# A decoder layer with an expert lookup on one core: three half sums in their own SBUF tile, and more gate, u and row buffers

## The chip, the core and the metric

The kernel runs on one core of one Trainium2 chip. The core has five engines that each take their own instructions strictly in order and signal each other through semaphores: TensorE (PE in the rows; PEld is its weight load), VectorE (DVE), ScalarE (ACT), GpSimd (POOL) and SyncE (SP, which here only issues DMAs). POOL issues DMAs too, the gathers by row number among them. The metric is device time in microseconds from start to end of one execution, the median of several; lower is better.

## The reference

One transformer layer over 1024 tokens of width 1024: modulated norm, windowed attention with a short convolution beside it, then a lookup of 16,384 experts, and a last norm. The lookup is what the change touches:

```python
def chunk(t):                                         # peer(), cut
    qh = (t @ w_q).reshape(T, 8, 2, 128)
    s = einsum('thpd,hpnd->thpn', qh, sub_keys)       # 2 x 128 scores a head
    s_top, i_top = top_k(s, 16)
    cand = s_top[:, :, 0, :, None] + s_top[:, :, 1, None, :]
    best, pos = top_k(cand, 16)                       # 16 of 256 pairs
    idx = take_along_axis(cand_idx, pos)              # rows of u_tab, v_tab
    g = softmax(best)
    act = gelu(einsum('thkd,td->thk', u_tab[idx], t))
    return einsum('thk,thkd->td', g * act, v_tab[idx])
...
x = x + g2 * peer(h2, ...);  return rmsnorm(x, final_g)
```

Each token takes 8 x 16 = 128 of the 16,384 rows of u_tab and v_tab.

## The kernel before

All matrix products are made in float16 pairs: a float32 operand is split into a high half (ACT, a scaled copy) and a low half (DVE, the rest), and `mm3` makes three matmuls of each product: high by high, high by low, low by high. Names ending in h and l (uh and ul, vh and vl, wdh and wdl) are such halves.

The run has three parts.

**The front** (up to about 1122 us): norms, projections, attention, convolution, mixing, and then, for each half of 512 tokens, the query projection and the top-k of the scores on DVE (`stage2`, `scores`; results in sv and si). While half 1 goes through `stage2`, the gates of half 0 are built beside it (`gates`): `select` finds the 16 pairs of each head, and `build_g` turns them into a dense table of gate values: DVE writes one-hot tiles e1, e2, ah, al of 8 tokens, `expand` multiplies them on PE, four tokens to a PSUM bank, ACT moves each bank into a tile ge (line 994), and each full ge goes to the table gd in DRAM. The weights of this part live in the pool wts, 24 KB per partition: four buffers whl and two w32 (`weight`). Its last user is the u part of chunks 3 to 5, which `run` splits ahead (`u_first`); their matmuls are `ups<-h,whl` in the rows.

**hf0** (about 1122 to 2580 us) takes half 0 densely against all experts, in 128 chunks of 128 experts (`chunk`). A chunk loads u (u32) and v (v32) from DRAM, splits them into uh, ul, vh, vl, multiplies uh and ul with the tokens (24 matmuls into a bank ups), applies the gelu (ACT, gel), multiplies by the gate values (DVE, `gel<-gel,gt`) and splits the product into wdh and wdl. Four chunks make a group; with the four v and w parts of one group `outputs` then makes eight blocks d of 128 output columns, two after each chunk of the next group. Blocks 0 to 4 keep their sums in PSUM for all of hf0; blocks 5 to 7 take a bank vps each time, which DVE adds to acc (`acc<-acc,vps`). Only three PSUM banks, v, serve vps, ups and the fbank of `expand`. The gate values come in as tiles gt, two for each block of 8 chunks (q 0 and 1, one for each half of the token blocks), loaded at the head of `chunk` with three buffers.

Beside hf0, `run_side` weaves in side work, a share after each step. It selects the pairs of the four quarters of half 1, and takes `dots` of each quarter: 128 gathered rows of u (POOL, `row`, four buffers), each multiplied with the token's own row and summed by one DVE instruction (`row<-row,hn`). It builds the gate table of the first three quarters.

**hf1** (about 2580 to 3110 us) takes those three quarters, 384 tokens, against v alone (their gates are already multiplied with the activations), chunk groups from the last to the first; the last quarter is summed from 128 gathered rows of v beside it (`rows_out`, racc). Then come the last norms and the output.

Pools stand on a left and a right stack. On the left, above the constants, the pool acc follows where wts has been, and the pool dense0 (gt, u32 and v32, uh, ul, vh, vl, wdl, gel) follows acc. A framework orders the instructions of each engine, places the tiles and inserts the semaphores: a tile that takes over another's memory waits for the last user of that.

Of the kernel before, what the change touches and what calls it, by code (L numbers as in the profile page):

```python
# [8 lines left out]
F32 = mybir.dt.float32  # L9
F16 = mybir.dt.float16  # L10
# [8 lines left out]
D = 1024  # L19
# [8 lines left out]
TB = 8  # L28
# [7 lines left out]
GR = 8  # L36
DVE_ROWS = ((), tuple(range(8)), (), (1, 2, 3, 4, 5, 7))
# [72 lines left out]
class K:  # L110
    def __init__(self, tc, a):
        self.tc = tc
        self.nc = Core(tc.nc)
        self.a = a
        self.wsplit = {}
        self.sel = {}
        self.ndots = {}
        self.nbank = 8
        self.nrstd = 3
        self.waiting = []  # L120
        self.turned = None
# [64 lines left out]
    def setup(self):  # L186
# [34 lines left out]
        self.sv = [None, pc.tile([128, 4, 2, 8, 16], F32, name="sv1")]  # L221
        self.si = [None, pc.tile([128, 4, 2, 8, 16], U32, name="si1")]
# [85 lines left out]
    def square(self, ps, k, x, p, n, tag="sq"):  # L308

        nc = self.nc  # L310
        sq = p.tile([128, n], F32, name=tag, tag=tag, bufs=self.nsq)
# [589 lines left out]
    def row(self, tab, ci, s):  # L901

        r = self.pg.tile([128, D], F32, name="row", tag="row", bufs=4)
# [48 lines left out]
    def build_g(self, t, hf):  # L952
# [7 lines left out]
        for q in range(128 // 16):  # L960
            ge = p.tile([128, 128, 16], F32, name="ge", tag="ge", bufs=self.ge_bufs)
            for sub in range(16 // TB):
# [3 lines left out]
                def onehot(name, src, idx, op):  # L966
                    x = p.tile([128, TB, 128 // REP, REP], F16, name=name, tag=name, bufs=2)
# [16 lines left out]
    def expand(self, t, hf, q, sub, ge, ah, al, e2):  # L984

        nc = self.nc
        for r in range(0, TB, 4):
# [6 lines left out]
            nc.scalar.activation(ge[:, :, o:o + 4].rearrange("p i t -> p t i"), ps, AF.Copy, scale=2.0 ** -12)  # L994
# [8 lines left out]
    def open_gate(self, name, side, ge_bufs):  # L1003
# [4 lines left out]
        io32 = p.tile([128, 128], F32, name="io32")  # L1008
# [65 lines left out]

    def chunk(self, hf, i1, p, pv):
# [5 lines left out]
        if self.gblock != (hf, i1 // GR):  # L1081
            self.gblock = hf, i1 // GR
            self.gts = []
            for q in range(2):
                gt = p.tile([128, nb, GR, 16], F32, name="gt", tag="gt", bufs=3)
                nc.sync.dma_start(
                    gt.rearrange("p b i t -> p b (i t)"),
                    self.gd[hf][nb * q:nb * q + nb].rearrange("b p i t -> p b (i t)")
                    [:, :, i1 // GR * GR * 16:(i1 // GR + 1) * GR * 16])
                self.gts.append(gt)  # L1090
# [51 lines left out]
    def outputs(self, hf, gi, d, chunks, acc, pv):  # L1142

        nc = self.nc
        nt = (NDENSE, NMIX)[hf]
# [11 lines left out]
        po = po[:, :nt]  # L1157
# [3 lines left out]
        ad = acc[:, d, :nt]  # L1161
        if keep:
            if last:
                nc.scalar.activation(ad, po, AF.Copy)
        elif first:
            nc.vector.tensor_copy(ad, po)
        else:
            nc.vector.tensor_add(ad, ad, po)
# [20 lines left out]
    def dense(self, p, pv, accs):  # L1189

        self.res, self.mix, self.vparts, self.gblock = {}, {}, {}, None
# [14 lines left out]
    def last_norm(self, ps, n, tag, p):  # L1206

        nc = self.nc
        r = p.tile([128, n], F32, name="rf", tag=tag, bufs=2)
# [86 lines left out]
    def experts(self, p, pv, acc0):  # L1296

        rows = self.rows_stream()
        accs = [acc0, None]
# [3 lines left out]
        accs[1] = self.pc.tile([128, 8, HALF], F32, name="acc1", tag="h2")  # L1303
        self.run_side(self.ends(main, acc0, p), rows=rows, rate=(128 + LATE_DOTS) / 374.0)
        for _ in rows:
            pass
        self.last_group(accs[1], p, pv)
# [10 lines left out]
    def run(self):  # L1318
# [60 lines left out]
        self.experts(pd, pv, acc0)  # L1379
# [68 lines left out]
```

## Time and profile before

| | us |
|---|---|
| three runs | 3127.59, 3132.65, 3133.32 |
| median of the runs | 3132.65 |
| the profiled execution | 3143.85 |
| its span, first to last instruction | 3142.1 |

| part of the span | length us | PE busy | DVE busy | DMA share |
|---|---|---|---|---|
| 600 to 1122, end of the front | 522 | 453.19 | 487.81 | 0.51 |
| 1122 to 1400, start of hf0 | 278 | 258.36 | 243.76 | 0.74 |
| 1400 to 2000, hf0 | 600 | 574.85 | 538.33 | 0.89 |
| 2000 to 2580, end of hf0 | 580 | 546.01 | 494.63 | 0.88 |
| 2580 to 3110, hf1 | 530 | 504.86 | 420.15 | 0.94 |

Length minus PE busy is the time in which no matmul ran. A row of waits names the engine and tile that waited, then who released it, then total, times and the longest.

### The profile page before, as it was taken

How to read it: one execution, taken by the hardware profiler on the slowest of the kernel's cores; microseconds unless marked ns; L12 is line 12 of the kernel's file. 1: busy time of each engine (PE TensorE's matmuls, PEld its weight loads, DVE VectorE, ACT ScalarE, POOL GpSimd, SP SyncE). 2: the span in 40 equal slices, each digit the busy share in tenths (PEclk: the TensorE clock that was granted, in tenths of full speed). 3: DMA queues.
4: the chain of work that ended last, by engine and by line, in shares of the span. 5: the costliest groups of instructions: out<-in, count | busy, mean ns of one | idle time of the engine just before them, and what ended most of it. 6: DMA issues, size and time to landing. Idle time of an engine off the chain costs nothing. (4 is left out here: it accounts for less than half of the span.)

```text
span 3142.1 us, 49200 instructions
## 1 busy us (share of the span) xinstructions
PE 2914.5 (93%) x18685; PEld 1537.5 (49%) x18685; DVE 2636.8 (84%) x5438; ACT 1269.8 (40%) x1878; POOL 1042.1 (33%) x812
## 2 busy tenths in 40 slices
PE   7899999988888989998999999899998999999998
PEld 2455555444444544443444444344444446666665
DVE  8788666699998998889898998889888988777787
ACT  4844566324555432322333332233433343433342
POOL 2100011201111005444444544445444444445453
PEclk9999999999999999999999999999999999999999
DMA  6233335653455628888899998889898979999996
GB/s 216 94 115 114 109 118 160 220 181 141 168 188 175 238 84 310 283 306 298 306 324 318 345 329 294 289 320 329 307 329 291 331 277 307 345 338 323 345 334 229
DMA packets 327197, 795.74 MB, mean 253 GB/s; under 512 B 22960, under 2 KB 147248, under 8 KB 319792
## 3 DMA queue, kind: packets, MB, share of 16 engines
q1 hardware_dynamic: 222992, 397.25, 37.7%
q0 software_dynamic: 103968, 395.36, 34.6%
q8 instruction: 146, 2.39, 0.3%
q14 instruction: 91, 0.75, 0.1%
HBM read 696.31 MB, written 96.21 MB: 252 GB/s over the span
## 5 line engine op out<-in xcount | busy, mean ns | idle before, releaser
L904 POOL DMA_INDIRECT row<-u,ci x512 | 684.7, 1337 | 931.3 <-DVE row L67 700.9
L67 DVE SCALAR_TENSOR_TENSOR row<-row,hn 128x1024 f32<-128x1024 f32 x512 | 619.1, 1223 | 83.3 <-DMA row<-u,ci 77.6
L67 PE MATMUL res<-wdl,vh 128*128 128x128 f16 (+2 forms) x2176 | 629.2, 306 | 20.6 <-DVE wdl L67 20.5
L67 PEld LDWEIGHTS <-vh 128*128 128x128 f16 x5120 | 469.0, 98 | 341.4 <-issue 11.2
L67 PE MATMUL res<-wdh,vh 128*128 128x128 f16 (+2 forms) x2176 | 625.3, 306 | 4.9 <-ACT vh L1109 3.0
L67 PE MATMUL res<-wdh,vl 128*128 128x128 f16 (+2 forms) x2176 | 625.6, 306 | 0.8 <-DVE vl L67 0.8
L67 PE MATMUL ups<-h,uh 128*128 128x512 f16 x1952 | 590.1, 384 | 28.1 <-DVE acc L67 14.9
L67 PEld LDWEIGHTS <-whl 128*128 128x128 f16 x3288 | 314.6, 99 | 408.1 <-issue 80.0
L1109 ACT ACTIVATE vh<-v 128x1024 f16<-128x1024 f32 x248 | 258.5, 1052 | 471.7 <-DMA v<-v 424.9
L67 PE MATMUL ups<-h,ul 128*128 128x512 f16 x976 | 375.3, 385 | 23.2 <-DVE ul L67 23.2
L67 PE MATMUL bank<-hT,whl 128*128 128x512 f16 x1584 | 374.3, 385 | 15.2 <-ACT hT L331 6.1
L67 PEld LDWEIGHTS <-vl 128*128 128x128 f16 x2560 | 251.5, 98 | 197.0 <-issue 29.0
L67 DVE SCALAR_TENSOR_TENSOR vl<-v,vh 128x1024 f16<-128x1024 f32 x248 | 299.5, 1219 | 55.2 <-ACT vh L1109 52.5
L67 PEld LDWEIGHTS <-uh 128*128 128x128 f16 x1952 | 192.9, 99 | 264.5 <-issue 43.6
L904 POOL DMA_INDIRECT row<-v,ci x128 | 197.5, 1543 | 214.4 <-DVE racc L67 190.5
L140 ACT ACTIVATE uh<-u 128x1024 f16<-128x1024 f32 x122 | 128.4, 1052 | 319.3 <-PE ups L67 259.1
L994 ACT ACTIVATE ge<-fbank 128x512 f32<-128x512 f32 x224 | 216.6, 1068 | 82.4 <-PE fbank L67 57.7
L1128 ACT ACTIVATE wdh<-gel 128x512 f16<-128x512 f32 x128 | 80.6, 631 | 358.1 <-DVE gel L67 335.8
L67 PE MATMUL fbank<-ah,e 128*128 128x128 f16 x896 | 131.4, 221 | 61.7 <-ACT ge L994 38.2
L67 DVE SCALAR_TENSOR_TENSOR racc<-row,fig,racc 128x1024 f32<-128x1024 f32 x127 | 162.7, 1281 | 6.6 <-DMA row<-v,ci 5.5
L67 DVE SCALAR_TENSOR_TENSOR ul<-u,uh 128x1024 f16<-128x1024 f32 x122 | 148.4, 1219 | 23.3 <-ACT uh L140 22.4
L67 DVE TENSOR_TENSOR e<-iotas,ii 128x1024 f16<-128x1024 f16 x224 | 150.8, 703 | 20.0 <-PE fbank L67 14.5
(230 smaller groups left out, 4118.6 us busy)
## 6 DMA issues: line engine op xcount, KB each, us to landing
v<-v SPq DMA_DIRECT2D x248, 512.0 KB
u<-u_t SPq DMA_DIRECT2D x122, 512.0 KB
gd<-ge POOLq DMA_DIRECT2D x32, 1024.0 KB
gt<-gd SPq DMA_DIRECT2D x32, 1024.0 KB
wm<-w_mod SPq DMA_DIRECT2D x48, 512.0 KB
gd<-ge SPq DMA_DIRECT2D x24, 1024.0 KB
gt<-gd SPq DMA_DIRECT2D x32, 768.0 KB
w<-w_in SPq DMA_DIRECT2D x34, 512.0 KB
```

Of the source, the lines that this page charges most:

```text
L67: r = f(*args, **kw)
L140: nc.scalar.activation(h, src, AF.Copy, scale=float(scale))
L904: self.nc.gpsimd.indirect_dma_start(out=r, out_offset=None, in_=tab, in_offset=bass.IndirectOffsetOnAxis(ap=ci[:, s:s + 1], axis=0))
L994: nc.scalar.activation(ge[:, :, o:o + 4].rearrange("p i t -> p t i"), ps, AF.Copy, scale=2.0 ** -12)
L1109: nc.scalar.activation(vh, v32, AF.Copy, scale=16.0)
L1128: nc.scalar.activation(wh, ge, AF.Copy, scale=256.0)
```

## The change

- **Half sums.** The tile acc0 of 16 KB per partition is gone from the pool acc. Blocks 5 to 7 are now summed in a tile part of 6 KB there, and the last addition of each writes to the whole tile, which is now made after the last chunk of hf0 in the place of h2, the tokens of half 0. acc1 follows in the same place after that.
- **Gate tiles.** `load_gates` is new. gt has four buffers, and the two tiles of the next block are asked for at the third and the sixth chunk of this one (`GATE_AT`).
- **u parts.** uh and ul have three buffers in place of two.
- **Row buffers.** Once the last quarter of half 1 is selected, each third gathered row takes the memory of sv1 or si1 in turn (`row`): six buffers in place of four.
- **Room and layout.** e1 has one buffer, io32 shares dot's. ACT's move of an expand bank reads it in the order (i, t) and so writes four neighbouring values at a time, where it read in the order of the bank and wrote single values 64 bytes apart.

Each engine executes the same instructions as before, apart from the shape of that move. The core of the diff:

```diff
         self.nrow += 1
+        if (1, 3) in self.sel and self.nrow % 3 == 0:
+            tag = ("sv1", "si1")[self.nrow // 3 % 2]
+            r = self.pc.tile([128, D], F32, name="row", tag=tag, bufs=1)
+        else:
+            r = self.pg.tile([128, D], F32, name="row", tag="row", bufs=4)
...
-                    x = p.tile([128, TB, 128 // REP, REP], F16, name=name, tag=name, bufs=2)
+                    x = p.tile([128, TB, 128 // REP, REP], F16, name=name, tag=name, bufs=1 if name == "e1" else 2)
...
-            nc.scalar.activation(ge[:, :, o:o + 4].rearrange("p i t -> p t i"), ps, AF.Copy, scale=2.0 ** -12)
+            nc.scalar.activation(ge[:, :, o:o + 4], ps.rearrange("p t i -> p i t"), AF.Copy, scale=2.0 ** -12)
...
+    def load_gates(self, hf, blk, q, p):
+        nb = (NDENSE, NMIX)[hf] // 32
+        if (hf, blk, q) not in self.gtiles:
+            gt = p.tile([128, nb, GR, 16], F32, name="gt", tag="gt", bufs=4)
+            self.nc.sync.dma_start(gt..., self.gd[hf]...)
+            self.gtiles[hf, blk, q] = gt
...
-        if self.gblock != (hf, i1 // GR):
...
+        nxt = blk - 1 if hf else blk + 1
+        if 0 <= nxt < 128 // GR:
+            for q in range(2):
+                if (i1 + hf * SUB) % GR == GATE_AT[q]:
+                    self.load_gates(hf, nxt, q, p)
...
-                uh = p.tile([128, 8, 128], F16, name="uh", tag="uh", bufs=2)
-                ul = p.tile([128, 8, 128], F16, name="ul", tag="ul", bufs=2)
+                uh = p.tile([128, 8, 128], F16, name="uh", tag="uh", bufs=3)
+                ul = p.tile([128, 8, 128], F16, name="ul", tag="ul", bufs=3)
...
+        ad = self.part[:, d - NRES, :]
         if first:
             nc.vector.tensor_copy(ad, po)
         else:
-            nc.vector.tensor_add(ad, ad, po)
+            nc.vector.tensor_add(acc[:, d, :] if last else ad, ad, po)
...
-        acc0 = self.pac.tile([128, 8, HALF], F32, name="acc0")
+        self.part = self.pac.tile([128, 8 - NRES, HALF], F32, name="part")
```

The order of the instructions moves in these places.

SP, end of the front and start of hf0, with the semaphores that each waits for (whl are weights of the front, w the u part of chunk 5, gt, v and gel the first tiles of hf0). Before:

```order
L157 DMA whl<-ws_wq_6775 128x2048 [waits DMAHW2_49,PE_49]
L800 DMA h2d<-hn 128x4x128 [waits DMAHW1_49,Activation_49]
L1086 DMA gt<-gd_92 128x16x128 [waits DMASW4_49,DMASW3_49,DMASW5_49,DMASW2_49,DMASW6_49,DMASW1_49,DMASW7_49,DMASW0_49,DVE_49]
L1086 DMA gt<-gd_92 128x16x128 [waits DMAHW3_49]
L800 DMA h2d<-hn 128x4x128 [waits DMAHW4_49,Activation_49]
L157 DMA whl<-ws_sk_6811 128x2048 [waits DMAHW5_49,PE_49]
L1106 DMA v_11999<-v 128x1024 [waits DMAHW6_49]
L1118 DMA gel<-ged_10238 128x512 [waits DMAHW7_49]
L157 DMA whl<-ws_wq_6853 128x2048 [waits DMAHW0_49,PE_49]
L1106 DMA v_12024<-v 128x1024 [waits DMAHW1_49]
```

After:

```order
L162 DMA w_11963<-u_t 128x1024 [waits DVE_49]
L1016 DMA io_11987<-iota 128x128 [waits DVE_49,DMAHW5_49,Activation_49,Pool_49]
L920 DMA hn_12442<-h2d 128x1024
L1087 DMA gt<-gd_92 128x16x128 [waits DMASW6_49,DMASW5_49,DMASW7_49,DMASW4_49,DMAHW1_49,DMASW3_49,DMAHW2_49,DMASW2_49,DMAHW3_49,DMASW1_49,DMAHW4_49,DMASW0_49,PE_49]
L1087 DMA gt<-gd_92 128x16x128
L1125 DMA v_11999<-v 128x1024
L1137 DMA gel<-ged_10238 128x512
L1125 DMA v_12024<-v 128x1024
L1137 DMA gel<-ged_10272 128x512
L1087 DMA gt<-gd_92 128x16x128 [waits DMAHW5_49]
```

The first loads of hf0 stood between the weights of the front; they now stand behind the last of them, behind io and hn, and the first gt names PE among what it waits for: it is the last of the 72 matmuls `ups<-h,whl`, the last reader of a buffer whl.

DVE, middle of hf0, with buffer numbers (row by row a sum of the dots, then the low halves of the next parts, then the gate product of chunk 81; a higher number is a later tile). Before:

```order
L67 SCALAR_TENSOR_TENSOR row_19248,dot_18584<-row_19248,hn2_18582 128x1024
L67 SCALAR_TENSOR_TENSOR wdl_19215<-gel_19216,wdh_19214 128x512
L67 SCALAR_TENSOR_TENSOR row_19251,dot_18584<-row_19251,hn2_18582 128x1024
L67 SCALAR_TENSOR_TENSOR row_19266,dot_18584<-row_19266,hn2_18582 128x1024
L67 SCALAR_TENSOR_TENSOR row_19282,dot_18584<-row_19282,hn2_18582 128x1024
L67 SCALAR_TENSOR_TENSOR vl_19377<-v32_19374,vh_19376 128x1024
L67 SCALAR_TENSOR_TENSOR vl_19464<-v32_19461,vh_19463 128x1024
L67 SCALAR_TENSOR_TENSOR ul_19458<-u32_19455,uh_19457 128x1024
L67 TENSOR_TENSOR gel_19298<-gel_19298,gt_19199 128x256
L67 TENSOR_TENSOR gel_19298<-gel_19298,gt_19201 128x256
```

After:

```order
L68 SCALAR_TENSOR_TENSOR row_19248,dot_18584<-row_19248,hn2_18582 128x1024
L68 SCALAR_TENSOR_TENSOR wdl_19215<-gel_19216,wdh_19214 128x512
L68 SCALAR_TENSOR_TENSOR row_19251,dot_18584<-row_19251,hn2_18582 128x1024
L68 SCALAR_TENSOR_TENSOR row_19266,dot_18584<-row_19266,hn2_18582 128x1024
L68 SCALAR_TENSOR_TENSOR row_19282,dot_18584<-row_19282,hn2_18582 128x1024
L68 SCALAR_TENSOR_TENSOR ul_19460<-u32_19457,uh_19459 128x1024
L68 SCALAR_TENSOR_TENSOR vl_19466<-v32_19463,vh_19465 128x1024
L68 SCALAR_TENSOR_TENSOR ul_19543<-u32_19540,uh_19542 128x1024
L68 TENSOR_TENSOR gel_19298<-gel_19298,gt_18682 128x256
L68 TENSOR_TENSOR gel_19298<-gel_19298,gt_18945 128x256
```

Ahead of the same gate product stood one ul; now there are two, and the second (ul_19543) belongs to the chunk after.

SP, middle of hf1, with buffer numbers (gt_25788 and gt_25790 before, gt_25455 and gt_25625 after, are the pair of the block that starts with the chunk whose v is v32_25792). Before:

```order
L1086 DMA gt_25375<-gd384_93 128x12x128
L1086 DMA gt_25788<-gd384_93 128x12x128
L1106 DMA v32_25521<-v 128x1024
L1106 DMA v32_25584<-v 128x1024
L1106 DMA v32_25623<-v 128x1024
L1106 DMA v32_25662<-v 128x1024
L1106 DMA v32_25723<-v 128x1024
L1106 DMA v32_25792<-v 128x1024
L1106 DMA v32_25831<-v 128x1024
L1106 DMA v32_25873<-v 128x1024
L1086 DMA gt_25790<-gd384_93 128x12x128
L1086 DMA gt_26206<-gd384_93 128x12x128
```

After:

```order
L1087 DMA gt_25455<-gd384_93 128x12x128
L1087 DMA gt_25625<-gd384_93 128x12x128
L1125 DMA v32_25523<-v 128x1024
L1125 DMA v32_25586<-v 128x1024
L1125 DMA v32_25627<-v 128x1024
L1125 DMA v32_25666<-v 128x1024
L1125 DMA v32_25727<-v 128x1024
L1125 DMA v32_25792<-v 128x1024
L1125 DMA v32_25831<-v 128x1024
L1125 DMA v32_25875<-v 128x1024
L1087 DMA gt_25873<-gd384_93 128x12x128
L1087 DMA gt_26043<-gd384_93 128x12x128
```

The second tile of the pair stood two v loads behind that chunk's own; now both stand five ahead of it.

## Rows read from the trace of the kernel before

**Rows 1.** Page: span, and busy time of the engines.

```profile
span 3142.1 us, 49200 instructions
PE 2914.5 (93%) x18685; PEld 1537.5 (49%) x18685; DVE 2636.8 (84%) x5438; ACT 1269.8 (40%) x1878; POOL 1042.1 (33%) x812
```

**Rows 2.** Windows: start:end, length, then busy us by engine, clock, DMA.

```profile
600.00:1122.00 522.00, 453.19 (x3064) 241.75 (x3063) 487.81 (x1769) 251.41 (x313) 57.59 (x69) 0.98 0.51 179
1122.00:1400.00 278.00, 258.36 (x1166) 114.99 (x1166) 243.76 (x614) 76.86 (x99) 105.69 (x79) 0.97 0.74 256
1400.00:2000.00 600.00, 574.85 (x2813) 265.93 (x2812) 538.33 (x968) 203.71 (x255) 278.62 (x210) 0.99 0.89 313
2000.00:2580.00 580.00, 546.01 (x2858) 261.80 (x2856) 494.63 (x797) 213.56 (x270) 254.37 (x192) 0.98 0.88 311
2580.00:3110.00 530.00, 504.86 (x4502) 348.56 (x4501) 420.15 (x588) 194.80 (x381) 251.86 (x166) 0.99 0.94 330
```

**Rows 3.** Waits of PE in hf0, 1140 to 2580 us: total, times, longest.

```profile
PE ups L67 <- DVE ul L67: 23.2, 6, 7.0
PE ups L67 <- DVE acc L67: 14.9, 7, 5.8
PE fbank L67 <- DVE acc L67: 14.2, 8, 7.0
```

**Rows 4.** Timeline of DVE: start, length, instruction, idle before it and its releaser.

```profile
1184.94 1.22 DVE L67 SCALAR_TENSOR_TENSOR row<-row,hn 128x1024 f32<-128x1024 f32 x1 [7.15 <-DMA row<-u,ci]
```

**Rows 5.** Timeline of PE around the start of hf0.

```profile
1120.64 0.29 PE L67 MATMUL bank<-whl,qql 128*128 128x128 f16 x1 [5.56 <-DVE qql L67]
1122.62 16.99 PE L67 MATMUL ups<-h,whl 128*128 128x512 f16 x72 [0.73 <-ACT sl L810]
...
1200.55 0.61 PE L67 MATMUL ups<-h,ul 128*128 128x512 f16 x1 [6.95 <-DVE ul L67]
```

**Rows 6.** Timeline of SP's queue: the first gate tiles.

```profile
1050.14 3.24 SPq L1086 DMA_DIRECT2D gt<-gd  x2
```

**Rows 7.** DMA in 1050 to 1060 us, when those tiles came in.

```profile
DMA packets 5235, 3.07 MB, mean 307 GB/s; under 512 B 74, under 2 KB 5116, under 8 KB 5234
```

**Rows 8.** Groups of DVE instructions: busy us, mean ns; idle before, releasers.

```profile
L67 DVE SCALAR_TENSOR_TENSOR vl<-v,vh 128x1024 f16<-128x1024 f32 x248 | 299.5, 1219 | 55.2 <-ACT vh L1109 52.5 <-PE res L67 1.4 <-issue 1.2
L67 DVE SCALAR_TENSOR_TENSOR ul<-u,uh 128x1024 f16<-128x1024 f32 x122 | 148.4, 1219 | 23.3 <-ACT uh L140 22.4 <-issue 0.8
L67 DVE TENSOR_TENSOR gel<-gel,gt 128x256 f32<-128x256 f32 x256 | 97.5, 419 | 13.9 <-ACT gel L1123 7.1 <-DMA gt<-gd 6.7
```

**Rows 9.** Groups of ACT instructions, moves of a PSUM bank.

```profile
L994 ACT ACTIVATE ge<-fbank 128x512 f32<-128x512 f32 x224 | 216.6, 1068 | 82.4 <-PE fbank L67 57.7 <-issue 13.1 <-DMA gd<-ge 7.4
...
L799 ACT ACTIVATE hn<-bank 128x512 f32<-128x512 f32 x8 | 4.8, 605 | 2.9 <-PE bank L67 2.9
```

**Rows 10.** Waits of PE at the end of the front, 600 to 1122 us.

```profile
PE fbank L67 <- ACT ge L994: 34.4, 53, 0.7
PE bank L67 <- DVE qql L67: 14.2, 13, 5.6
```

**Rows 11.** Waits of DVE in the same stretch.

```profile
DVE e L67 <- PE fbank L67: 11.9, 20, 0.8
```

**Rows 12.** Waits of PE in hf1, 2580 to 3110 us.

```profile
PE res L67 <- DVE wdl L67: 20.3, 14, 2.7
```

**Rows 13.** Waits of DVE in hf1.

```profile
DVE wdl L67 <- ACT wdh L1135: 63.5, 14, 8.0
```

**Rows 14.** Waits of ACT in hf1.

```profile
ACT vh L1109 <- DMA v<-v: 159.3, 65, 10.8
ACT wdh L1135 <- DMA gt<-gd: 105.9, 15, 10.4
```

**Rows 15.** Tile ci, the row numbers that a selection gives: first and last start.

```profile
L67 DVE SCALAR_TENSOR_TENSOR ci<-fig x4: 284/285/286, 1175.8 to 1992.6; 128x128 int32<-128x128 f32 x4
```

**Rows 16.** Waits of DVE in 2000 to 2580 us.

```profile
DVE row L67 <- DMA row<-u,ci: 31.6, 23, 3.6
```

More of the change, by code (lines that the diff above doesn't have):

```diff
@@ L220, in setup @@
         self.h2h, self.h2l = [None, None], [None, None]
-        self.sv = [None, pc.tile([128, 4, 2, 8, 16], F32, name="sv1")]
-        self.si = [None, pc.tile([128, 4, 2, 8, 16], U32, name="si1")]
+        self.sv = [None, pc.tile([128, 4, 2, 8, 16], F32, name="sv1", tag="sv1")]
+        self.si = [None, pc.tile([128, 4, 2, 8, 16], U32, name="si1", tag="si1")]
         self.h2d = self.tc.dram_tile([4, 128, D], F32, name="h2d")
@@ L310, in square @@
         nc = self.nc
-        sq = p.tile([128, n], F32, name=tag, tag=tag, bufs=self.nsq)
+        sq = p.tile([128, n], F32, name=tag, tag=tag, bufs=3 if tag == "uh" else self.nsq)
         nc.scalar.activation(sq, x, AF.Square)
@@ L901, in row @@
     def row(self, tab, ci, s):
-        r = self.pg.tile([128, D], F32, name="row", tag="row", bufs=4)
+        self.nrow += 1
+        if (1, 3) in self.sel and self.nrow % 3 == 0:
[3 more added lines that the diff above has]
+            r = self.pg.tile([128, D], F32, name="row", tag="row", bufs=4)
         self.nc.gpsimd.indirect_dma_start(out=r, out_offset=None, in_=tab,
@@ L1007, in open_gate @@
         p = self.pg
-        io32 = p.tile([128, 128], F32, name="io32")
+        io32 = p.tile([128, 128], F32, name="io32", tag="dot", bufs=1)
         nc.sync.dma_start(io32, a["iota"])
@@ L1080, in chunk @@
         hh, hl = self.h2h[0], self.h2l[0]
-        if self.gblock != (hf, i1 // GR):
-            self.gblock = hf, i1 // GR
-            self.gts = []
+        blk = i1 // GR
+        if self.gblock != (hf, blk):
+            self.gblock = hf, blk
             for q in range(2):
[L1085 to L1090, printed above, removed]
+                self.load_gates(hf, blk, q, p)
+            self.gts = [self.gtiles.pop((hf, blk, q)) for q in range(2)]
+        nxt = blk - 1 if hf else blk + 1
[3 more added lines that the diff above has]
+                    self.load_gates(hf, nxt, q, p)
         early = hf == 0 and i1 < UPRE
@@ L1160, in outputs @@
                      i == SUB - 1 and (last or not keep))
[L1161 removed]
         if keep:
             if last:
[L1164 to L1165 removed]
+                nc.scalar.activation(acc[:, d, :], po, AF.Copy)
+            return
+        ad = self.part[:, d - NRES, :]
+        if first:
             nc.vector.tensor_copy(ad, po)
         else:
[L1168 removed]
+            nc.vector.tensor_add(acc[:, d, :] if last else ad, ad, po)
     def outputs_mix(self, first, last, d, chunks, pv):
@@ L1208, in last_norm @@
         nc = self.nc
-        r = p.tile([128, n], F32, name="rf", tag=tag, bufs=2)
+        r = p.tile([128, n], F32, name="rf", tag=tag, bufs=3 if tag == "ul" else 2)
         nc.scalar.activation(r, ps, AF.Sqrt, bias=self.eps, scale=1.0 / D)
@@ L1294, in last_group, with whole_acc, experts @@
                 nc.sync.dma_start(ov[:, k - 1:k + 1, HALF:HALF + NMIX], acc[:, k - 1:k + 1, :NMIX])
-    def experts(self, p, pv, acc0):
+    def whole_acc(self, name):
+        return self.pc.tile([128, 8, HALF], F32, name=name, tag="h2")
+    def experts(self, p, pv):
         rows = self.rows_stream()
-        accs = [acc0, None]
+        accs = [None, None]
         main = self.dense(p, pv, accs)
@@ L1302, in experts @@
         self.run_side(islice(main, steps), self.gates_stream(), GATES_D, rows, (512 - LATE_DOTS) / (steps - 15.0), (1, 0))
-        accs[1] = self.pc.tile([128, 8, HALF], F32, name="acc1", tag="h2")
-        self.run_side(self.ends(main, acc0, p), rows=rows, rate=(128 + LATE_DOTS) / 374.0)
+        accs[0] = self.whole_acc("acc0")
+        self.run_side(self.ends(main, accs[0], p), rows=rows, rate=(128 + LATE_DOTS) / 374.0)
         for _ in rows:
             pass
-        self.last_group(accs[1], p, pv)
+        self.last_group(self.whole_acc("acc1"), p, pv)
     def ends(self, main, acc0, p):
```

12 lines of the change are left out of this document (8 added, 4 removed).

## Prediction

> **What bounds the kernel now.** Read first the span and the busy times [rows 1]: PE is busy for 2914.5 of 3142.1 us, so 228 us at most can be won by waiting less, and no instruction is taken away. Then read the stretches [rows 2]. Length minus PE busy is 68.8 us at the end of the front, 19.6 and 25.2 and 34.0 us in the three stretches of hf0, and 25.1 us in hf1. In the front DVE is the fuller engine (487.81 of 522 us busy). In hf0 both are nearly full: in 1400 to 2000 PE is busy for 96% and DVE for 90%. In hf1 DMA stands beside PE: share 0.94.
>
> Then ask what ended PE's waits. In hf0 it is nearly always DVE [rows 3]: the low half ul late by 23.2 us in all, and the additions that free the PSUM banks late by 14.9 and 14.2 us. DVE itself is rarely short of work. It takes its instructions in order, and one that stands still holds all behind it: at 1184.94 it had waited 7.15 us for a gathered row [rows 4], and the next ul then came 6.95 us late for PE [rows 5]. In hf1 one chain runs through three engines: ACT waits 105.9 us for gate tiles [rows 14], DVE 63.5 us for ACT's wdh [rows 13], PE 20.3 us for DVE's wdl [rows 12]; the difference is what two groups of buffers absorb.
>
> **The change, part by part.** The sum is made against the profiled execution, 3143.85 us; the median of the runs is 3132.65, that is 11.2 us lower, and these are taken off at the end.
>
> *Gate eviction.* The same 224 moves of an expand bank, 128 of them in the front. Now each takes 1068 ns [rows 9], where a move of a bank with plain order on both sides takes 605 ns. The new form writes runs of four values, but reads four places of a bank 128 values apart. No row shows such a read. The bounds: 605 ns, if only the scattered writing cost time; and 1068 + 463 = 1531 ns, if reading apart costs as much again and adds to it. I take 605, since the row that differs from the plain one differs in the writing alone. What it brings: in the front PE waits 34.4 us for these moves [rows 10], and DVE 11.9 us for PE to be done with its one-hot tiles [rows 11]. DVE is the fuller engine there, so its 11.9 us are the limit and PE's 34.4 are not: I take 10 us. At 1531 ns the 128 moves of the front would add 59 us to ACT. That is as much slower as 605 is faster, so PE's wait would at most double, by 34.4 us; DVE's idle time there (522 - 487.81 = 34 us) takes up some of it, and I bound the loss at 25 us.
>
> [...] The row shows only that writing single values apart costs 463 ns more than the plain move [rows 9]. [...] No row here shows a read of PSUM with a step.
>
> *Less room in the pool acc.* part is 10 KB smaller than acc0 was, so dense0 begins 10 KB lower, inside what was wts, and its first tiles, the first two gt, wait for the last reader of that memory. By the order this is the last of the 72 matmuls with the weights of chunks 3 to 5, and behind these two gt in SP's queue stand the first v, gel and u. Before, the first gt went out at 1050.14 us [rows 6], and PE came through the start without a gap. Now nothing of hf0 is loaded until these matmuls end, at 1122.62 + 16.99 = 1139.6 us on the old clock [rows 5].
>
> That gives and takes. It gives: eight vl, two ul and four gate products (8 x 1.219 + 2 x 1.219 + 4 x 0.419 = 13.9 us of DVE [rows 8]) leave the end of the front, where PE waited for DVE's qql, 5.56 us of it at the very end [rows 5, 10]. So PE ends the front some 7 us sooner, near 1132.5. It takes: two gate tiles of 1 MB, v and gel are 2.9 MB, at the 307 GB/s of the rows [rows 7] 9 to 10 us, so PE's first output of hf0 starts near 1144 rather than at 1140.4; and DVE, which stands still for those 10 us, has the 13.9 us of work still to do, while the first selection of half 1 (36 us from 1139.6 to its ci at 1175.8 [rows 15]) is woven in. By the order the ul of chunk 6 stands behind five chunks' vl and gate products (5 x 2.06 = 10 us) and more than half of that selection (some 22 us): near 1176. PE has 108 matmuls of outputs ahead of it, at 16.99/72 us each [rows 5] 25 us, and needs it at 1169. In the order ul now leads the gate product by only one or two chunks through the first 25 chunks (two or three before). So PE stops again at each of the next parts and runs 10 to 25 us late at first. DVE then sets the pace, and regains a part, because PE's old waits of this time (19.6 us up to 1400 [rows 2]) exist only where PE is early. Net I take 10 us lost; bounds: 0, if the selection takes up all the slack, and 20, the moved 13.9 plus the waits for the first rows (7.15 [rows 4]) less nothing regained.
>
> *Third u pair.* From about chunk 25 on ul stands three or four chunks ahead of the gate product in DVE's order, before two or three. A chunk is about 11 us of PE (48 matmuls at 16.99/72 us [rows 5]), so a hold-up such as that of 7.15 us no longer reaches PE by ul. What is late next are the additions on the same queue, 29.1 us in all of hf0 [rows 3], which the change does not move.
>
> *Fourth gate tile, loads a block ahead.* Within hf0 this takes away hold-ups of DVE of 6.7 us [rows 8]. In hf1 it takes away the whole chain at its head: the second tile of a pair is now asked for six chunks sooner, and its 15 waits of ACT are in the main over.
>
> *Two more rows.* Only once the last selection is done, at 1992.6 us [rows 15]. From there to 2580 DVE waited 31.6 us for rows [rows 16], and PE 34.0 in all. In hf1 DVE hardly waits for rows.
>
> *Hf0 from 1400 on.* PE's gaps are 25.2 + 34.0 = 59.2 us [rows 2]. ul, the gate tiles, the cheaper move and the deeper rows act on the same gaps, so they are priced together: I take a third, 20 us; bounds 5 and 40. *Hf1.* Of the 20.3 us I take 12, since v is waited for by ACT as well (159.3 us [rows 14]) and the DMA share of 0.94 leaves 6% of 530 us, 32 us, to be shared; bounds 0 and 20.
>
> *Nothing:* e1 with one buffer (writer and readers are all on DVE, in the same order as before), io32, the new place of acc0 and acc1 (both used after h2 is dead).
>
> **Sum.** 10 - 10 + 20 + 12 = 32 us. 3143.85 - 32 = 3111.9, less 11.2: 3101 us.
>
> **The rivals.**
>
> *The eviction does not get cheaper* (reading PSUM in steps costs what the scattered writing did): ACT stays at 1068 ns, PE's 34.4 us in the front stay, and the sum is 22 us: 3111. At the upper bound it is 10 us lost, not won, and 25 more: 3101 + 35 = 3136. For it: the reading apart is new. Against: nothing in the rows but the writing explains the 463 ns. [...]
>
> *DMA holds hf1.* With the gate tiles early, v comes late in their place, and PE waits for vh. Then 12 us are missing: 3113. For it: share 0.94, and ACT's 159.3 us for v. Against: 20.3 of PE's 25.1 us there are waits for wdl, and the bytes are the same.
>
> *The start is not made up* (slower than before). PE is 20 us late after the first ten chunks; DVE, 90% full afterwards, has no slack to regain it, and from 1400 on the gaps merely change their name from ul to acc, since the additions stand on the same queue. Front and hf0 then bring 0, hf1 6: 3132.65 + 20 - 6 = 3147. It decides from a loss at the start of 12 us, if the rest brings no more than that. For it: 29.1 us of PE's waits are already for the additions. Against: DVE's hold-ups by rows and gate tiles shrink too.
>
> *The row buffers do nothing.* POOL's gathers wait for DVE to free a row, not the other way round; then a few of the 20 us are missing, inside the bounds.
>
> **How the numbers follow.** The forecast as summed, 3070 to 3118: 0.47. Eviction not cheaper: 0.23, of it 0.15 below 3126. DMA holds hf1: 0.12, of it 0.09 below 3126. Start not made up: 0.18, of it 0.16 above 3139. About 0.2% (6 us, so 3126 and 3139) is what a measurement of this kernel can tell from no change. Faster: 0.47 + 0.15 + 0.09 = 0.71, taken as 0.69 for the tails of the forecast. Slower: 0.16, and 0.03 from an eviction at its upper bound: 0.19. Same: 0.12. The range reaches from all bounds of hf0 and hf1 at their best (3101 - 28 - 8 = 3065) to the start not made up: 3065 to 3148.
>
> **What would show it.** The group of the gate moves near 605 ns, and PE's wait for it in the front gone. The first gt on SP's queue near 1132, PE's first output of hf0 some 10 us behind it, and PE's gaps between 1122 and 1400 above 25 us. PE's waits for ul after 1400 gone, those for acc not. In hf1 no wait of ACT for gt, and PE's for wdl below 8 us. The forecast is wrong if the move takes over 1068 ns, if PE's waits for acc grow by more than 20 us, or if hf1 is no shorter than 525 us.

## The result, and the profile after

The changed kernel takes 3159.99 us (median of 4 runs, 3156.53 to 3161.2) against 3132.73 of the kernel before (median of 4 runs, three of them those of the table above): ratio 1.0080, 95% interval 1.0059 to 1.0102. Repeated later in 6 runs it took 3159.12, ratio 1.0074 (1.0050 to 1.0098). It is 27 us slower; the forecast was 3101, and the range ended at 3148. Of all the runs below one was slow, at 3750 us and a mean granted clock of 0.75; it is left out of stage4's median, which is 3080.8 with it and 3078.1 without.

Page of the changed kernel, span and busy time, as in [rows 1]:

```profile
span 3158.6 us, 49130 instructions
...
PE 2930.6 (93%) x18685; PEld 1533.7 (49%) x18685; DVE 2636.2 (83%) x5438; ACT 1186.9 (38%) x1878; POOL 1041.7 (33%) x812
```

Windows by stage, as in [rows 2] (start:end, length, busy us of PE, PEld, DVE, ACT, POOL, granted clock, DMA share, GB/s). The stages end where its own do: the front at 1118, hf0 at 2605.

```profile
1118.00:1400.00 282.00, 237.38 (x1026) 102.78 (x1027) 228.57 (x521) 83.58 (x103) 99.55 (x75) 0.92 0.79 271
1400.00:2000.00 600.00, 557.59 (x2719) 257.33 (x2718) 516.01 (x942) 185.41 (x247) 264.36 (x201) 0.98 0.87 303
2000.00:2605.00 605.00, 582.49 (x3035) 277.41 (x3034) 534.67 (x868) 204.52 (x289) 280.63 (x211) 0.98 0.90 319
2605.00:3128.00 523.00, 501.64 (x4488) 347.12 (x4488) 415.09 (x583) 193.38 (x378) 238.00 (x159) 0.99 0.92 328
```

PE's gaps are 44.6, 42.4, 22.5 and 21.4 us; before they were 19.6, 25.2, 34.0 and 25.1. So the loss lies in the first 880 us of hf0. The work is the same. Timeline of PE, with the idle time before an instruction, and of SP's queue with the first gt:

```profile
1100.14 17.77 PE L68 MATMUL ups<-h,whl 128*128 128x512 f16 x72 [0.73 <-ACT sl L812]
1130.10 1.01 PE L68 MATMUL res<-wdh,vh 128*128 128x512 f16 x2 [12.18 <-ACT wdh L1147]
...
2605.01 0.48 PE L68 MATMUL res<-wdh,vh 128*128 128x384 f16 x1 [4.41 <-ACT wdh L1154]
...
1117.95 1.40 SPq L1087 DMA_DIRECT2D gt<-gd  x2
```

From such rows each kernel below is cut into three lengths: the front, to the end of the 72 ups matmuls; hf0, to the first matmul of 384 columns; hf1, to the end of the span. Before: 1139.6, 1445.0 and 557.5 us. After: 1117.9, 1487.1 and 553.6. The front gained 22 us, where 10 for the eviction and 7 for the moved work were forecast; hf0 lost 42; hf1 gained 4. These are lengths of one execution each, and that of the kernel before was 11 us above its median. Of the 42 us of hf0, 30.5 are more idle time of PE (109.6 us against 79.1), and 11.6 more busy time for the same matmuls (1377.5 against 1365.9), at a mean granted clock of 0.97 instead of 0.98.

Waits in hf0 of the changed kernel, 1118 to 2600 us, of PE, DVE and ACT:

```profile
PE ups L68 <- DVE part L68: 35.3, 17, 3.9
PE res L68 <- ACT wdh L1147: 18.8, 4, 12.2
PE ups L68 <- ACT uh L142: 17.0, 6, 9.1
PE ups L68 <- DVE ul L68: 7.6, 1, 7.6
PE fbank L68 <- DVE part L68: 5.0, 2, 3.7
...
DVE ul L68 <- ACT uh L142: 75.7, 41, 6.9
DVE row L68 <- DMA row<-u,ci: 63.9, 41, 8.5
...
DVE wdl L68 <- ACT wdh L1147: 5.0, 4, 2.2
...
ACT uh L142 <- DMA u<-u_t: 303.6, 85, 12.5
ACT uh L142 <- PE ups L68: 148.9, 26, 7.7
```

The same two waits of ACT in hf0 of the kernel before (1140 to 2580 us), which the prediction did not read, and three of DVE:

```profile
ACT uh L140 <- PE ups L67: 259.1, 58, 7.6
...
ACT uh L140 <- DMA u<-u_t: 59.2, 25, 5.0
...
DVE wdl L67 <- ACT wdh L1128: 35.6, 10, 9.0
DVE ul L67 <- ACT uh L140: 22.4, 17, 2.5
DVE vl L67 <- ACT vh L1109: 21.8, 10, 5.9
```

PE's waits for ul fell from 23.2 [rows 3] to 7.6 us, as meant. But ACT's uh, which waited for PE to free a pair, now waits for its load, and DVE waits 75.7 us for uh where it waited 22.4. DVE's waits for wdh fell at the same time; for the three halves together (uh, vh at 24.9, wdh) they rose from 79.8 to 105.6 us. What is then late on DVE's queue are the additions into part: they hold up ups by 35.3 us where [rows 3] has 14.9, and ups and fbank together by 40.3 where it has 29.1.

In hf1 the waits for the gate tiles are gone (2.7 us instead of the 105.9 of [rows 14]), and nothing is won. ACT and DVE, 2605 to 3159 us:

```profile
ACT vh L1128 <- DMA v<-v: 258.3, 75, 13.4
...
DVE vl L68 <- ACT vh L1128: 91.6, 20, 10.0
```

The 159.3 us for v [rows 14] became 258.3, and DVE's 63.5 for wdh [rows 13] became 91.6 for vh.

### The profile page after: what moved, and what is told of

It reads as the page before. It is cut to its first block, busy times and chain, and to the rows that moved or that the text cites. A ratio compares the mean times of both kernels' runs of the same rounds, so it can differ in the third digit from the quotient of the medians.

```text
span 3158.6 us, 49130 instructions
## 1 busy us (share of the span) xinstructions
PE 2930.6 (93%) x18685; PEld 1533.7 (49%) x18685; DVE 2636.2 (83%) x5438; ACT 1186.9 (38%) x1878; POOL 1041.7 (33%) x812
## 4 chain that ended last, share of the span: by engine, by line
DVE 19%; issue 16%; DMA 15%; PE 15%; POOL 7%; ACT 2%; SPq 0%; DVEq 0%; POOLq 0%; ACTq 0%
DMA v<-v 8%; POOL row L911 7%; PE res L68 6%; PE ups L68 5%; DVE row L68 4%; DMA row<-u,ci 4%; DMA u<-u_t 3%; DVE vl L68 2%; PE vps L68 2%; DVE wdl L68 2%; DVE racc L68 1%; DVE e L68 1%; DVE eq L68 1%; DVE si L68 1%; PE bank L68 1%
## 5 line engine op out<-in xcount | busy, mean ns | idle before, releaser
L68 PE MATMUL ups<-h,uh 128*128 128x512 f16 x1952 | 590.7, 385 | 60.0 <-DVE part L68 35.3
L68 PEld LDWEIGHTS <-uh 128*128 128x128 f16 x1952 | 192.3, 99 | 298.4 <-issue 59.2
L142 ACT ACTIVATE uh<-u 128x1024 f16<-128x1024 f32 x122 | 128.9, 1056 | 454.8 <-DMA u<-u_t 303.6
L68 DVE SCALAR_TENSOR_TENSOR ul<-u,uh 128x1024 f16<-128x1024 f32 x122 | 149.0, 1222 | 78.1 <-ACT uh L142 75.7
L68 PEld LDWEIGHTS <-ul 128*128 128x128 f16 x976 | 96.6, 99 | 128.2 <-DVE ul L68 9.7
L68 PE MATMUL vps<-wdh,vh 128*128 128x512 f16 x384 | 147.9, 385 | 10.0 <-ACT gel L1142 4.0
```

Source lines behind the costliest of these rows:

```text
L68: r = f(*args, **kw)
L142: nc.scalar.activation(h, src, AF.Copy, scale=float(scale))
```

## The experiments

Two theories. **Staging**: u and v come through three tiles of 4 KB (tag uv32), the staging tiles, and a load can start only when DVE has split an earlier one. With a third u pair the split of u stands earlier in the queues, ahead of its load, and ACT and DVE stand still; early gate tiles only uncover the same shortage in hf1. **Late start**: dense0 begins 10 KB lower, inside wts, and hf0 pays for it. The rivals ask of each part whether it does anything.

Waits of SP's queue for such a tile in the changed kernel, 1140 to 2580 us (L1116 loads u, L1125 v):

```profile
SPq L1116 <- DVE vl L68: 375.8, 81, 21.3
SPq L1125 <- DVE ul L68: 284.8, 79, 19.6
```

In the kernel before the same waits are 183.6 us for u and 278.2 for v. "Late start" below names the layout of the changed kernel; "low" the one in which the u pairs lie in acc, so that dense0 begins above wts.

| kernel | start | u pairs | staging | gates | us | ratio to before (95%) | front, hf0, hf1 |
|---|---|---|---|---|---|---|---|
| before_evict | as before | 2 | 3 | late | 3123.0 | 0.9972 (0.9958 to 0.9986) | 1129.8, 1434.1, 554.8 |
| low_two_block | low | 2 | 3 | late | 3125.6 | 0.9970 (0.9953 to 0.9988) | 1128.8, 1454.9, 552.5 |
| late_two_block | late | 2 | 3 | late | 3143.3 | 1.0024 (1.0010 to 1.0038) | 1115.5, 1474.7, 558.2 |
| low_two | low | 2 | 3 | early | 3131.9 | 0.9994 (0.9975 to 1.0012) | 1126.6, 1458.9, 555.3 |
| two_pairs | late | 2 | 3 | early | 3149.9 | 1.0059 (1.0039 to 1.0079) | 1119.2, 1472.5, 552.8 |
| block_gates | late | 3 | 3 | late | 3163.6 | 1.0086 (1.0058 to 1.0115) | 1115.4, 1493.4, 558.6 |
| low_u | low | 3 | 3 | early | 3143.9 | 1.0039 (1.0022 to 1.0056) | 1121.1, 1464.2, 546.3 |
| four_rows | late | 3 | 3 | early | 3162.7 | 1.0100 (1.0067 to 1.0132) | 1115.1, 1482.2, 558.1 |
| changed | late | 3 | 3 | early | 3160.0 | 1.0080 (1.0059 to 1.0102) | 1117.9, 1487.1, 553.6 |
| stage4_block_gates | late | 2 | 4 | late | 3116.4 | 0.9935 (0.9914 to 0.9956) | 1114.7, 1442.4, 556.4 |
| pairs3_stage4 | late | 3 | 4 | late | 3116.9 | 0.9940 (0.9919 to 0.9962) | 1116.9, 1440.4, 556.4 |
| stage4 | late | 2 | 4 | early | 3078.1 | 0.9832 (0.9804 to 0.9859) | 1115.6, 1435.6, 525.1 |
| low_u_stage4 | low | 2 | 4 | early | 3091.0 | 0.9868 (0.9838 to 0.9899) | 1119.2, 1442.4, 525.8 |
| low_u_stage6 | low | 2 | 6 | late | 3087.0 | 0.9852 (0.9822 to 0.9882) | 1123.0, 1400.6, 547.4 |
| stage6_gt | late | 2 | 6 | early in hf1 | 3064.5 | 0.9788 (0.9763 to 0.9812) | 1118.5, 1420.7, 523.6 |
| low_u_stage6_gt | low | 2 | 6 | early in hf1 | 3057.3 | 0.9744 (0.9722 to 0.9766) | 1128.1, 1408.1, 525.8 |

The lengths are of one profiled execution each, the times medians. A profiled execution can lie far from its median (low_two_block's took 3138.0 us, low_u's 3133.4, low_u_stage6's 3072.8), so a difference of times between rows goes by the ratios, and one of lengths is rough.

**before_evict.** The kernel before, with this alone:

```diff
-            nc.scalar.activation(ge[:, :, o:o + 4].rearrange("p i t -> p t i"), ps, AF.Copy, scale=2.0 ** -12)
+            nc.scalar.activation(ge[:, :, o:o + 4], ps.rearrange("p t i -> p i t"), AF.Copy, scale=2.0 ** -12)
```

> The kernel before with the new order of the gate eviction alone. If the 22 us by which the front became shorter come from the cheaper move (592 against 1068 ns), the last of the 72 ups matmuls ends near 1118 to 1125 instead of 1139.6 us, and the time falls by 10 to 25 us against before, to 3108 to 3123. If they come from the vl, ul and gate products that left the front, the end of the front moves by less than 8 us and the time by less than 10.

The front ends 9.8 us sooner, the time falls by 9.8: between the two cases of the expectation. The other 12 us of the changed kernel's shorter front go with DVE work that left it: DVE is busy for 924.4 us up to the front's end, 937.8 before. How much that work is worth one profile cannot tell: in five pairs of kernels that differ in the layout alone (low_two_block and late_two_block, low_two and two_pairs, low_u and changed, low_u_stage4 and stage4, low_u_stage6_gt and stage6_gt) the late one's front ends 13.3, 7.4, 3.2, 3.6 and 9.6 us sooner.

**low_u, low_two_block, late_two_block.** In the two low ones the u pairs go into the pool acc (for the two-pair form part is padded by one block, so that acc is still 24 KB):

```diff
-                uh = p.tile([128, 8, 128], F16, name="uh", tag="uh", bufs=3)
-                ul = p.tile([128, 8, 128], F16, name="ul", tag="ul", bufs=3)
+                uh = self.pac.tile([128, 8, 128], F16, name="uh", tag="uh", bufs=3)
+                ul = self.pac.tile([128, 8, 128], F16, name="ul", tag="ul", bufs=3)
```

> The changed kernel with the three pairs of u parts moved from dense0 into the pool acc, beside part and wdh: acc then is 26 KB, dense0 begins above the whole of wts, and the first gate tiles, v and gel can be loaded in the front as before the change. Nothing else differs. Theory B (late start): the first gt goes out near 1050 instead of 1118 us, PE's wait of 12.2 us at the start of hf0 and the moved DVE work go away, and the time falls by 20 to 30 us, to 3130 to 3140; the front may give back some of its 22 us. Theory A: at most 10 us fall, to 3150 or more, since the waits after 1250 remain.

> The changed kernel with two u pairs, three gate tiles asked for at the block's start, and dense0 above wts (the pool acc holds part, padded by one block, wdh and the u pairs). What is left of the change is the gate eviction, the two extra rows, e1 with one tile and part apart from acc0. If these others cost nothing, the time is that of before with the new eviction alone, 3123 within 5 us; if one of them costs, 3130 to 3140.

> As low_two_block, but the u pairs in dense0 and no padding, so that dense0 begins inside wts and hf0 starts late. The late start by itself: 16 us slower than low_two_block if it costs the same without the third pair (from 3160 against 3144), less than 8 if the two hide each other.

low_u is 13 us faster than the changed kernel by the ratios (1.0080 - 1.0039 of 3133; 16 by the medians), late_two_block 17 us slower than low_two_block, and two_pairs 20 us slower than low_two: with three staging tiles the late start costs 13 to 20 us with either number of pairs. For low_u that lies between what its two theories gave. PE's first matmul of hf0 (timeline) and the 6 us from there (window, columns as above), in low_two_block:

```profile
1129.52 1.02 PE L68 MATMUL res<-wdh,vh 128*128 128x512 f16 x4 [0.77 <-ACT wdh L1147]
```

```profile
1129.00:1135.00 6.00, 5.34 (x25) 2.34 (x25) 5.32 (x16) 5.46 (x8) 0.00 (x0) 1.00 0.44 124
```

The same in late_two_block:

```profile
1127.77 1.01 PE L68 MATMUL res<-wdh,vh 128*128 128x512 f16 x2 [12.25 <-ACT wdh L1147]
```

```profile
1128.00:1134.00 6.00, 5.94 (x19) 2.14 (x18) 6.00 (x27) 3.89 (x5) 0.00 (x0) 0.65 0.85 256
```

PE stood still for 12.25 us, and then ran its first 6 us at a mean granted clock of 0.65, where the other kernel had 1.00. Over the whole of hf0 PE's busy time is nevertheless the same, 1374.8 us here and 1374.6 there; the 19.7 us by which hf0 is longer are idle time (99.9 against 80.4), so the cost of the late start does not show as a lower clock over the stage. low_two_block also equals before_evict by the ratios (0.9970 and 0.9972), so the parts costed at nothing (e1, io32, the place of acc0), with the extra rows, together cost nothing that can be measured.

**two_pairs, pairs3_stage4, stage4_block_gates, block_gates.** The edits for two pairs instead of three, for a fourth staging tile and for gate loads at the block's start, which the table combines (uh as ul, and u32 as v32):

```diff
-                ul = p.tile([128, 8, 128], F16, name="ul", tag="ul", bufs=3)
+                ul = p.tile([128, 8, 128], F16, name="ul", tag="ul", bufs=2)
-            v32 = p.tile([128, D], F32, name="v32", tag="uv32", bufs=3)
+            v32 = p.tile([128, D], F32, name="v32", tag="uv32", bufs=4)
-            gt = p.tile([128, nb, GR, 16], F32, name="gt", tag="gt", bufs=4)
+            gt = p.tile([128, nb, GR, 16], F32, name="gt", tag="gt", bufs=3)
-        if 0 <= nxt < 128 // GR:
+        if False:
```

> The changed kernel with two pairs of u parts again, everything else of the change kept. Theory A (the third pair is what costs in hf0: with it ul stands earlier in DVE's queue, before its u has landed, since u still has only the three staging tiles): DVE's waits for uh, 75.7 us in hf0 after the change, fall towards the 22.4 us of before, PE waits for ul again as in [rows 3], and the time falls by 10 to 20 us, to 3140 to 3150. Theory B (the late start of hf0 is the whole loss): the time stays at 3160, within 5 us. Theory C (the third pair does what it was priced at): without it PE's waits grow and the time rises by 5 to 15 us, to 3165 to 3175.

> The changed kernel with three gate tiles, asked for at the start of a block as before; all else of the change kept. If the early gate loads bring what they were priced at, their loss costs 5 to 15 us in hf1 and the time is 3165 to 3175. If with three staging tiles they only move the wait from gt to v (105.9 us of ACT's waits for gt before, 258 us for v after), hf1 stays within 4 us of 553.6 and the time within 5 us of 3160. If they hold back v and u on SP's queue, the time falls by 5 us or more.

> The changed kernel with three u pairs kept, three gate tiles asked for at the block's start (as in block_gates, 3164 us), and a fourth staging tile in a part of the room so freed. If the third pair only did harm because the loads had no fourth staging tile, the time falls by 50 us or more against block_gates, to 3085 to 3110. If the third pair itself is what holds hf0 (by the order that it gives DVE and ACT), the time falls by less than 30 us, to 3135 or more.

> The kernel stage4 with three gate tiles, asked for at the block's start as before. With three staging tiles the early gate loads brought 0 to 4 us. If with four they are what lets hf1 come down to 525 us, hf1 grows to 540 to 558 and the time to 3095 to 3115. If the fourth staging tile alone did that, the time stays at 3076 to 3088. Against pairs3_stage4, which has a third u pair more and is otherwise the same, it shows the price of that pair where loads have four tiles: a gain if pairs3_stage4 is faster by more than 6 us, nothing if within 6.

With three staging tiles the third pair costs 7 us (changed against two_pairs) to 19 us (block_gates against late_two_block); with four tiles and late gates it neither costs nor brings (0.9940 against 0.9935). pairs3_stage4 is 46 us below block_gates, nearer to the 50 or more of "no fourth staging tile" than to the 30 at most of "the pair itself". block_gates came out within the 5 us of 3160 that its second case gave, its hf1 1 us beyond; stage4_block_gates has the long hf1 of its first case, at a time 1 us above its range. In hf0 of two_pairs DVE's waits for uh and ACT's for PE and u are back near the old:

```profile
DVE ul L68 <- ACT uh L142: 27.3, 20, 3.6
...
ACT uh L142 <- PE ups L68: 249.2, 52, 8.8
ACT uh L142 <- DMA u<-u_t: 91.4, 36, 12.8
```

One place of the changed kernel shows how it costs: SP's queue, then ACT, then DVE.

```profile
1490.68 0.33 SPq L1125 DMA_DIRECT2D v<-v  x1
...
1506.32 0.33 SPq L1125 DMA_DIRECT2D v<-v  x1
1515.86 0.33 SPq L1116 DMA_DIRECT2D u<-u_t  x1
...
1522.23 1.06 ACT L142 ACTIVATE uh<-u 128x1024 f16<-128x1024 f32 x1 [5.05 <-DMA u<-u_t]
1523.20 1.99 ACT L1128 ACTIVATE vh<-v 128x1024 f16<-128x1024 f32 x2
...
1514.56 1.23 DVE L68 SCALAR_TENSOR_TENSOR ul<-u,uh 128x1024 f16<-128x1024 f32 x1
...
1524.27 1.23 DVE L68 SCALAR_TENSOR_TENSOR vl<-v,vh 128x1024 f16<-128x1024 f32 x1 [4.20 <-ACT vh L1128]
```

The load of u had been waiting in SP's queue for a staging tile. It goes out at 1515.86, right after DVE has finished an older ul (1514.56 + 1.23), and lands 6.4 us later. uh stands still for it, and two vh stand behind uh in ACT's queue. Their loads are the last two of v before that, which went out at 1490.68 and 1506.32, the first of them 32 us before its vh; DVE waits 4.20 us for this vh.

**stage4.** Two pairs, four staging tiles (the same memory), early gates.

> The changed kernel with two pairs of u parts and, in the 4 KB so freed, a fourth staging tile for u and v. Theory A (the staging tiles bound the loads): u and v are asked for one load sooner, DVE's waits for uh and vh (75.7 and 24.9 us in hf0, 91.6 us for vh in hf1 after the change) fall below half, hf1 comes out 5 to 15 us shorter than 562 us, and the time falls by 20 to 40 us against the changed kernel, to 3120 to 3140. Theory B (late start alone): 3155 to 3160. A third possibility, that DMA bandwidth and not the tiles holds v back: DVE's waits for vh in hf1 stay above 80 us and hf1 at 560.

3078 us: by the ratios 78 below the changed kernel and 53 below the one before, where 20 to 40 below the changed one were expected. Waits of ACT in its hf1, and a window (columns as above) from its first matmul to 3046 us:

```profile
ACT vh L1128 <- PE res L68: 259.7, 27, 9.8
...
ACT vh L1128 <- DMA v<-v: 11.4, 4, 9.2
```

```profile
2551.00:3046.00 495.00, 494.77 (x4492) 346.62 (x4492) 415.20 (x583) 186.31 (x379) 250.47 (x160) 1.00 0.95 347
```

ACT now waits for PE, and PE is busy for 494.77 of 495 us. With four staging tiles and late gates (stage4_block_gates) ACT waits for gt again:

```profile
ACT wdh L1154 <- DMA gt<-gd: 123.4, 15, 12.2
```

So hf1 has two shortages side by side. With two pairs and the late start, its length is 558.2 us with neither mended (late_two_block), 552.8 with early gates, 556.4 with four staging tiles, 525.1 with both. The early gates alone change the whole time by +11 us (late_two_block to two_pairs, 1.0024 to 1.0059), the staging tile alone by -28, both by -60. The early gates gain 43 us with four staging tiles (0.9935 to 0.9832) and lose 11 with three. Of the halved DVE waits that were expected of stage4 the one for uh came (30.9 us); those for vh were a miss: 27.6 us in hf0, and still 71.5 in hf1, but no longer late for PE.

**low_two.** As low_two_block, with early gates.

> As low_two_block, with the fourth gate tile and the gate loads a block ahead. If with three staging tiles the early gate loads only move the wait, the time is that of low_two_block within 5 us. If they disturb the u and v loads of hf0 on SP's queue, it is 5 to 15 us above it.

0.9994 against 0.9970, intervals that overlap: at most a few us lost. In late_two_block and two_pairs the loss of 11 us is clear of the errors, while from block_gates to the changed kernel it is not there (1.0086 to 1.0080). What the early loads push aside in hf0 is not settled.

**four_rows.** The row buffers of the dead top-k tiles left out:

```diff
-        if (1, 3) in self.sel and self.nrow % 3 == 0:
+        if False:
```

> The changed kernel with four row buffers throughout. The two more act only from the last selection on, some 500 us of hf0. If they bring the 20 us by which the changed kernel catches up there (it is 43 us late at the 80th vl and 16 us late at the 128th), the time rises by 10 to 25 us, to 3170 to 3185. If they do nothing, it stays within 5 us of 3160.

Nothing that can be measured. The changed kernel does catch up after 2000 us, but this one too: from there to the end of hf0 PE makes 5.02 matmuls a microsecond in the changed kernel, 5.01 in this one and 4.92 before. Waits of DVE for rows from 2000 to 2580 us, in the changed kernel and in this one:

```profile
DVE row L68 <- DMA row<-u,ci: 3.6, 4, 2.0
...
DVE row L68 <- DMA row<-u,ci: 28.3, 24, 3.7
```

The two buffers do what they were put in for (31.6 us before [rows 16]), and the time does not change.

**low_u_stage4, low_u_stage6, low_u_stage6_gt, stage6_gt.** Toward a better kernel. Six staging tiles (in the low ones one of them, as the fourth in low_u_stage4, with a tag of its own in acc) take the memory of the fourth gate tile and the third pair; the fourth gate tile of hf1 uses part's memory, dead there:

```diff
-            gt = p.tile([128, nb, GR, 16], F32, name="gt", tag="gt", bufs=4)
+            self.ngt += hf
+            if hf and self.ngt % 4 == 0:
+                gt = self.pac.tile([128, nb, GR, 16], F32, name="gt", tag="part", bufs=1)
+            else:
+                gt = p.tile([128, nb, GR, 16], F32, name="gt", tag="gt", bufs=3)
-        if 0 <= nxt < 128 // GR:
+        if hf and nxt >= 0:
```

> Both mendings at once: two pairs of u parts and the fourth staging tile (as in stage4), and the u pairs and the fourth staging tile placed in the pool acc beside part and wdh, so that dense0 begins above wts (as in low_u). If late start and staging are separate causes, their gains add: hf0 loses the 22.9 us by which low_u's is shorter than the changed kernel's (1464.2 against 1487.1), and the time is near 3081 - 16 - 5 = 3060, 3055 to 3068. If the fourth staging tile already makes up for the late start, the time stays at 3075 to 3085.

> As low_u_stage4, but the 8 KB of the fourth gate tile go into two more staging tiles, six in all, and the gate tiles are three again and asked for at the start of their block. If DVE's remaining waits for uh and vh (30.9 and 27.6 us in hf0, 71.5 in hf1 with four staging tiles) are waits for loads, six tiles take most of them away and the time falls by 5 to 15 us below low_u_stage4. If the gate tiles asked for late hold hf1 as before (63.5 us of DVE's waits in [rows 13]), hf1 is 10 to 25 us longer than with four and four, and the time is 10 to 20 us above low_u_stage4.

> As low_u_stage6, and in half 1 a fourth gate tile in the memory of part, which is dead there (6 KB each), with the gate tiles of the next block asked for at chunks 3 and 6; half 0 loads them at the block's start. If hf1 needs both the staging tiles and the early gate loads, it is 525 us as in stage4 instead of 547.4, and the time 3087 - 22 = 3065, 3055 to 3072. If the staging tiles alone set hf1, it stays at 547 and the time at 3083 to 3090.

> As low_u_stage6_gt, but the u pairs and all staging tiles lie in dense0 as in the changed kernel, so that dense0 begins inside wts and hf0 starts late. If the late start costs by itself the 22.9 us that low_u showed against the changed kernel, hf0 is longer by 20 to 25 us and the time is 15 to 20 above low_u_stage6_gt. If deeper staging makes it up, as the pair of stage4 (3081) and low_u_stage4 (3091) hints, the time is within 8 us of low_u_stage6_gt or below it.

low_u_stage4 was a miss: the gain of low_u was not there again, and the intervals of stage4 and low_u_stage4 overlap. With six tiles the low layout is ahead by 14 us by the ratios, 7 by the medians, and the intervals touch. So what the late start costs where the loads have more tiles is not settled. low_u_stage6 shows both cases of its expectation at once: against low_u_stage4 hf0 is 42 us shorter and hf1 22 longer, and the time is the same within the intervals. Six tiles shorten hf0 to 1400 to 1421 us, and hf1 needs the early gates besides. low_u_stage6_gt takes 3057.3 us, as expected, 0.9744 of the kernel before and the fastest of all.

**after_again.** The changed kernel unaltered, run together with low_two_block, late_two_block and low_two.

> The changed kernel once more, beside the three above on the same chip: 3160 if the 27 us are its own, 3145 to 3155 if its first 4 runs lay high.

3159.12 us. A way from before to after in single steps, by the ratios: new eviction -0.28%, parts costed at nothing and rows -0.02%, early gates +0.24%, third pair +0.45%, late start +0.41%. That makes +0.80%, 25 of the 27 us, as it must, since each step starts where the last one ends; in another order the steps have other sizes (the third pair 7 to 19 us, the late start 13 to 20, the early gates from 2 us gained to 11 lost).

## Why the prediction was wrong

- *Gate eviction*: right, 10 us forecast, 9.8 measured. The move takes 592 ns where 605 was taken; the rival that it does not get cheaper, at 0.23, did not come about, and no row shows a price of the stepped read. Group of the moves in the changed kernel:

```profile
L1001 ACT ACTIVATE ge<-fbank 128x512 f32<-128x512 f32 x224 | 121.9, 592 | 88.5 <-PE fbank L68 73.1 <-DMA gd<-ge 6.5 <-issue 6.1
```

- *Less room in the pool acc*: the mechanism right, the size off. The first gt went out at 1117.95 behind the 72 matmuls, and PE stopped for 12.18 us. (The forecast for that gt, near 1132, left out the 10 us that the prediction itself gave the front for the eviction.) The moved work shortens the front by 3 to 13 us, 7 in the mean of the five pairs, as forecast. The net loss is 13 to 20 us where 10 was taken, at the upper end of the bounds of 0 to 20 (whose own terms, 13.9 and 7.15, make 21). It wasn't made up later, as the rival *the start is not made up* had it; but at 3147 that rival still gave hf1 6 us and had no loss by the third pair.
- *Third u pair*: the step that failed. The prediction saw PE wait for ul, and saw in the order that ul came earlier, and took that for a gain. It never asked what ul waits for. ACT's 259.1 us of waits for PE in hf0 meant that uh had its load in hand; with one pair more they fell to 148.9, and the waits for u rose from 59.2 to 303.6. The load of u waits for a staging tile, of which there are still three. The sign was wrong: 7 to 19 us lost with three tiles, nothing with four (and late gates).
- *Fourth gate tile*: the chain of [rows 12 to 14] is there, and this step failed too: its removal brought at most 5 us of the 12 in hf1 (3 longer in low_two against low_two_block), since ACT's 159.3 us for v, named in the same group, stood beside it. This is what the rival *DMA holds hf1* describes, v late in the gates' place, for a wrong reason: the share of 0.94 was no limit, since with four staging tiles 347 GB/s were moved, at a share of 0.95, where [rows 2] has 330. In the whole time the early loads cost 11 us with two pairs (7 in the low layout, not clear of the errors) and nothing with three; what they push aside in hf0 is open.
- *Two more rows* and *Nothing*: worth nothing. The rows' waits went, so that this is worth nothing has another reason than the rival *the row buffers do nothing* gave; which one is open. The 20 us of *hf0 from 1400 on*, priced together, were a loss: PE's gaps there grew from 59.2 to 64.9 us, the waits for ul fell and those for the additions rose, which was named as next in line but not priced.

Of the 42 us of gains in the sum, the 10 of the eviction were real; the two other gains were losses or nothing, and the one loss was larger than taken. The range's lower end, 3101 - 28 - 8, counts hf1's 8 us twice, for the 28 are 20 of hf0 and these 8; nothing hangs on it.

## What to carry to other kernels

Before a buffer is added, follow the wait of the engine that it serves back to the load, and ask which tile that load itself waits for; here 4 KB given to the staging tile instead of a third output pair turned +25 us into -53, by the ratios. Where two chains of loads feed the same engine, neither shortage need show its worth alone (here +11 and -28 us singly, -60 together): mend both in one trial before either is dropped. When a pool shrinks, look at what now lies on the memory of the stage before, and put there what is needed last.

## What the runs showed of the hardware that was not expected

A move of a PSUM bank that reads four places 512 bytes apart and writes runs of 16 bytes takes 592 ns in the changed kernel; plain moves of a bank by ACT take 591 (sl<-bank) and 601 (hn<-bank) in the same profile. The stepped read shows no price there. So all of the 463 ns over the plain move (1068 against 605 [rows 9]) lay in writing single values 64 bytes apart. DMA moved 347 GB/s over 495 us in stage4.
